# The first projections of a hybrid layer by halves of the sequence: eight plain output tiles instead of six, low parts of their weights by accumulating DMA

## The chip, the cores and the metric

One core of one Trainium2 chip runs the whole kernel. The time is device microseconds for one execution, the median of several runs. Engines are called as in the profile: PE (TensorE, matrix products), ACT (ScalarE), DVE (VectorE), POOL (GpSimd) and SP (SyncE, which here only issues loads). Each engine works through its own instructions in order and waits on semaphores. SP, ACT and POOL each issue DMAs into a queue of their own; all queues are served by the same 16 DMA engines.

## What is computed

A layer of a hybrid network on a sequence of 1024 rows of 1024 values. The change is in its beginning:

```python
c_act = jax.nn.silu(c)
mod = (c_act @ w_ada[i] + b_ada[i]).reshape(bsz, N_MOD, D_MODEL)[:, :, None, :]
shift1, scale1, gate1 = mod[:, 0], mod[:, 1], mod[:, 2]
u = rms_norm(x, ln1[i]) * (1.0 + scale1) + shift1
proj = u @ w_in
gl, cb, cc, cx, z, xbc, dt = jnp.split(proj, split_at, axis=-1)
...
g_conv, g_ssm = jnp.split(jax.nn.sigmoid(gl), 2, axis=-1)
```

`gl` are the first 2048 columns of the input projection: 16 output tiles of 128 columns, f = 0 to 15. Everything behind them (the other projections, a short convolution, a state-space scan, the output projections and an MLP) is the same in both kernels.

## The kernel before

**Data.** x comes transposed: 8 blocks k of 128 channels, each in two halves h of 512 rows of the sequence (tile `x{k}{h}`, 128x512, 256 KB). A weight tile `win[f]` is 128x1024 (512 KB), its columns k*128 to k*128+127 being the block for k. For each k, two tiles of `wada1` (512 KB each, tile `wada`) give, by a product-and-sum with the activated conditioning row on DVE (`gemv`, two records each: the custom instruction and the read of its accumulator), the scale column (q=1) and the shift column (q=0) of that k in `mcol`.

**Precision.** Each product is made of three fp32r matmuls: high weight by high u, high weight by low u, low weight by high u. `load_w` makes the high weight by a cast on ACT (`whi`) and the low one by a subtraction on DVE (`wlo`). `shift_split` does the same for u: ACT writes `uh` = x + shift, rounded; DVE writes `ul`, the rest.

**The head**, from the start to the last plain product:

- SP loads the conditioning row and the parameters, the first halves of x for all k, the first two `wada` tiles, the second halves of x, and then weights and `wada` tiles by turns. `wraw` has three buffers, `wada` eight.
- ACT squares both halves of all k, DVE adds them up, PE sums over channels (`st`), DVE takes the inverse root (the root: `rsqrt_eps` and the diagonal `sdg`), PE spreads it to all partitions, ACT copies it (`rb0`, `rb1`).
- Then for j = 0 to 7 (j is the k whose turn it is): two `gemv`, the column `s1c`, x times `s1c` times `rb` for both halves (line 46 of the kernel, `x<-x,s1c,rb`), `shift_split` for both halves, and 24 matmuls: four weight tiles f = 0 to 3, two halves, three products. Their eight sums fill the eight PSUM banks (four of pool `mm`, two each of `sx` and `st`).
- ACT writes tanh of each sum to `glt` and stores it to `gl_d`.
- Tiles f = 4 and 5 follow as plain products by `proj`, 96 matmuls.

All other tiles of the kernel that read u in pairs go by `strassen_pair`: seven half-size products of 12 matmuls each, 84 for a pair of output tiles instead of 96, with sums of weights (`s12`, `s34`) and of u (`tops_of`, made on DVE behind the head) as operands. f = 6 to 15 are five such pairs. Between f = 5 and the first pair stands the stage for dt: 32 matmuls with `wd`, 16 small ones with `sel`, an evacuation, and then the pair.

**Order.** The program is traced line by line; a list scheduler with its own estimate of durations may move instructions of an engine, also DMA issues. `tc.issue_after` holds single pieces back.

Of the kernel before, what the change touches and what calls it, by code (L numbers as in the profile page):

```python
# [37 lines left out]
def hybrid_trunk(tc, xT, par, hrows, crow, wada1, wada2, win, wdt, wco, wso, wo, wup, wdt_, wdn, out):  # L38
# [223 lines left out]
    crw = glp.tile([1, T], F32, name="crw", tag="glt")  # L262
    sp.dma_start(crw, crow)
    sp.dma_start(prm, par)
    for h in (0, 1):
# [2 lines left out]
        act.activation(ct[:, hs[h]], ps, AF.Tanh, scale=0.5)
# [31 lines left out]
    warm(4, xt[0][0])  # L300
    st = ps0.tile([P, H], F32, name="st")
    for h in (0, 1):
        acc = None
        for k in range(KT):
            sq = p0.tile([P, H], F32, name="ssq" if k else "sacc", bufs=4 if k else 2)
            act.activation(sq, xt[k][h], AF.Square)
# [4 lines left out]
        for j in range(4):
            pe.matmul(st[:, 4 * h + j:4 * h + j + 1], lhsT=acc[:, j * P:j * P + P], rhs=ones[:, 0:1],
                      start=h == j == 0, stop=True, skip_group_check=True)
    warm(2, acc)
    r = rsqrt_eps(p0, st[:, 0:8], 1.0 / T, [P, 8], "nst")
    rbs = []
    for h in (0, 1):
# [757 lines left out]
```

## Time and profile before

| | |
|---|---|
| median of 3 runs | 2132.69 us (2129.87 to 2138.76) |
| the profiled execution | 2131.68 us, span of its instructions 2129.9 us |
| PE busy | 2090.5 us, 98% of the span |
| DVE, ACT, POOL busy | 69%, 44%, 7% |
| first matmul of a plain tile starts | 32.38 us |
| first matmul of the first Strassen pair starts | 105.45 us |
| granted TensorE clock, mean of the span | 0.989 |
| accumulating DMAs in the old kernel | 36 of 256 KB, from 1818 us on |

In rows of the timeline the columns are start and busy time in us, engine, line and operation, output and inputs, shapes and count; in square brackets stands how long the engine had been idle before, and what ended it. In the table of stretches each engine has its busy time and, in brackets, its count of instructions; the last three columns are the granted clock, the share of time in which the 16 DMA engines were busy, and GB/s. Rows of DMA queues give packets, MB and the share of time of the 16 engines; q1 is SP's queue, q0 is POOL's.

### The profile page before, as it was taken

The numbers are of one execution on the slowest core, as the hardware profiler recorded it, in microseconds if no ns is written. First come the engines' busy times: TensorE is split into PE (matmuls) and PEld (weight loads), VectorE is DVE, ScalarE is ACT, GpSimd is POOL, SyncE is SP. The second block draws the span as 40 slices with busy tenths as digits, with TensorE's granted clock in tenths as the row PEclk, the third lists the DMA queues.
The fourth block names the chain that finished last, engine by engine and source line by source line (L and its number), as shares of the span: only waits on it lengthen the run. The fifth ranks groups of instructions, "written<-read, shape, count | busy, mean of one in ns | idle before, by whom it ended". The sixth has DMA issues, their size and how long they took to land.

```text
span 2129.9 us, 26252 instructions
## 1 busy us (share of the span) xinstructions
PE 2090.5 (98%) x9776; PEld 1705.4 (80%) x9776; DVE 1474.1 (69%) x2278; ACT 928.4 (44%) x1554; POOL 152.1 (7%) x242
## 2 busy tenths in 40 slices
PE   7999999999999999999999999999999999999997
PEld 4778888888888887888877788888888887888887
DVE  7866888664786757577786558746866664668774
ACT  4433333224565646364664331224544444454432
POOL 0000000000000000000000000012000001231213
PEclk8999999999999999999999999999999999999998
DMA  8126554123133223232347586453144446988922
GB/s 307 74 99 205 188 190 161 67 79 122 59 102 117 75 93 91 85 115 81 103 124 282 178 301 200 170 189 114 60 163 163 163 178 234 281 242 255 283 73 80
DMA packets 133617, 327.32 MB, mean 154 GB/s; under 512 B 12481, under 2 KB 47681, under 8 KB 131954
## 3 DMA queue, kind: packets, MB, share of 16 engines
q1 hardware_dynamic: 98978, 202.76, 29.4%
q0 software_dynamic: 22240, 87.04, 12.7%
q10 hardware_dynamic: 12272, 35.85, 4.3%
q8 instruction: 77, 1.26, 0.2%
q14 instruction: 50, 0.41, 0.1%
HBM read 253.05 MB, written 72.55 MB: 153 GB/s over the span
## 4 chain that ended last, share of the span: by engine, by line
PE 78%; issue 14%; DVE 4%; DMA 3%; ACT 1%; POOL 1%; SPq 0%; DVEq 0%; POOLq 0%; ACTq 0%
PE mm L146 20%; PE mm L112 13%; PE mm L115 13%; PE mm L113 13%; PE mm L969 11%; PE B L602 1%; PE B L607 1%; DMA wv<-in_wada 1%; PE C L624 1%; DMA y<-x_d 1%; DVE wada L293 1%; POOL wv L417 1%; PE A L579 1%; DVE ul L46 1%; DVE x L46 0%
## 5 line engine op out<-in xcount | busy, mean ns | idle before, releaser
L112 PE MATMUL mm<-uh,whi 128*128 128x512 f32 x768 | 302.9, 398 | 4.1 <-ACT uh L105 3.6
L113 PE MATMUL mm<-ul,whi 128*128 128x512 f32 x768 | 304.4, 396 | 0.0
L146 PE MATMUL mm<-t,whi 128*128 128x512 f32 x944 | 291.1, 390 | 0.6 <-DVE cq L43 0.6
L115 PE MATMUL mm<-uh,wlo 128*128 128x512 f32 x768 | 246.3, 396 | 1.9 <-DVE wlo L43 1.9
L95 ACT CAST whi<-wraw 128x1024 fp32r<-128x1024 f32 x101 | 106.0, 1050 | 261.4 <-PE mm L113 206.5
L43 DVE TENSOR_TENSOR wlo<-wraw,whi 128x1024 fp32r<-128x1024 f32 (+1 forms) x167 | 186.4, 1117 | 40.2 <-ACT whi L95 34.1
L146 PEld LDWEIGHTS mm<-t,whi 128*128 128x128 f32 x944 | 177.3, 188 | 39.2 <-DVE cq L43 2.5
L969 PE MATMUL mm<-op,whi 128*128 128x512 f32 x672 | 207.0, 389 | 0.0
L146 PE MATMUL mm<-t,wlo 128*128 128x512 f32 x472 | 183.0, 389 | 0.0
L112 PEld LDWEIGHTS mm<-uh,whi 128*128 128x128 f32 x768 | 144.4, 189 | 36.3 <-ACT uh L105 5.7
L115 PEld LDWEIGHTS mm<-uh,wlo 128*128 128x128 f32 x768 | 144.5, 189 | 32.0 <-DVE wlo L43 2.3
L113 PEld LDWEIGHTS mm<-ul,whi 128*128 128x128 f32 x768 | 145.1, 189 | 29.4 <-issue 0.9
L112 PE MATMUL mm<-ys,whi 128*128 128x512 f32 x384 | 148.7, 397 | 1.6 <-DVE gt L46 1.1
L43 DVE TENSOR_TENSOR wlo<-s,whi 128x1024 fp32r<-128x1024 f32 (+1 forms) x114 | 111.9, 994 | 54.5 <-ACT whi L151 53.6
L113 PE MATMUL mm<-ys,whi 128*128 128x512 f32 x384 | 148.5, 395 | 0.0
L969 PEld LDWEIGHTS mm<-op,whi 128*128 128x128 f32 x672 | 126.1, 188 | 26.3
L46 DVE SCALAR_TENSOR_TENSOR cacc<-raw,hw,cacc 128x1024 f32<-128x1024 f32 x96 | 122.8, 1279 | 27.6 <-ACT cacc L554 27.2
L146 PE MATMUL mm<-s,whi 128*128 128x512 f32 x448 | 138.3, 389 | 0.7 <-ACT cu L169 0.7
L969 PE MATMUL mm<-op,wlo 128*128 128x512 f32 x336 | 130.7, 389 | 0.0
L596 ACT ACTIVATE seg<-acb,acum 128x128 f32<-128x128 f32 x256 | 81.9, 392 | 99.5 <-PE B L602 91.9
L46 DVE SCALAR_TENSOR_TENSOR y<-mm,mcol,y 128x512 f32<-128x512 f32 (+1 forms) x100 | 69.6, 705 | 76.8 <-PE mm L969 41.4
L115 PE MATMUL mm<-ys,wlo 128*128 128x512 f32 x384 | 121.9, 392 | 0.0
(280 smaller groups left out, 4078.2 us busy)
## 6 DMA issues: line engine op xcount, KB each, us to landing
wraw<-in_win SPq DMA_DIRECT2D x87, 512.0 KB, 3.5
dr<-in_wdt_ SPq DMA_DIRECT2D x108, 256.0 KB, 5.1
op_d<-hp POOLq DMA_DIRECT2D x12, 1792.0 KB, 6.2
hr<-op_d POOLq DMA_DIRECT2D x42, 512.0 KB, 5.8
wv<-in_wada POOLq DMA_DIRECT2D x32, 512.0 KB, 3.7
acb<-ac_d SPq DMA_DIRECT2D x64, 256.0 KB, 4.5
wraw<-in_wup SPq DMA_DIRECT2D x32, 512.0 KB, 3.5
gt<-gl_d SPq DMA_DIRECT2D x24, 512.0 KB, 5.0
```

The lines of the kernel that those rows point to most:

```text
L43: return eng.tensor_tensor(out=o, in0=a, in1=b, op=op)
L46: return dve.scalar_tensor_tensor(out=o, in0=a, scalar=s, in1=b, op0=op0, op1=op1)
L95: act.copy(hi, raw)
L112: pe.matmul(o, lhsT=wh, rhs=h_, start=start, stop=False)
L113: pe.matmul(o, lhsT=wh, rhs=l_, start=False, stop=False)
L115: last_mm[0] = pe.matmul(o, lhsT=wl, rhs=h_, start=False, stop=stop)
L146: last_mm[0] = pe.matmul(o, lhsT=l_[:, s_], rhs=r_, start=first and k == j == 0, stop=k == 3 and j == 2, skip_group_check=True)
L293: return dve.tensor_tensor_reduce(out=w_, in0=w_, in1=cb, scale=0.5, scalar=prm[:, BADA + o:BADA + o + 1], op0=ALU.mult, op1=ALU.add, accu ...
L417: pool.dma_start(w_, wada2[i])
L579: pe.matmul(A[:, 0:P], lhsT=bf[:, cs], rhs=cf[:, cs], start=True, stop=True)
L596: act.activation(seg[:, r, :], acb[:, r, :], AF.Relu, bias=acum[:, c, hd:hd + 1], scale=-1.0)
L969: pe.matmul(o, lhsT=l_[:, c_], rhs=t[:, r_, k, :], start=first and k == j == 0, stop=k == 3 and j == 2, skip_group_check=True)
```

## The change

Eight plain tiles, f = 0 to 7, instead of six; the pairs begin at f = 8. The first halves of the sequence go first, for all eight tiles, whose eight sums fill the eight banks; the second halves of f = 4 to 7 follow k by k in the banks of f = 0 to 3 (pool `mm`), and then the second halves of f = 0 to 3. SP loads the first halves of x and leaves the second ones to step j = 1. The inverse root is taken for each half apart. The low weight is no longer a subtraction: ACT writes the rounded weight a second time, with its sign turned, and POOL adds the weight to it from HBM by an accumulating DMA. Weights of f = 4 to 7 lie in a pool of their own, `p0w`; `wada` has four buffers instead of eight. Matmuls of 128x128 on a tile of ones (`warm`) stand between PE's first steps. At the end of the head each instruction of PE, ACT, DVE and SP is tied to the one before it on its engine, so that the scheduler keeps the order of the text. `gemvs(4)` in two pairs takes the place of `gemvs(3)` in three.

```diff
+    p0w = tc.alloc_tile_pool(name="p0w", bufs=4)
...
+    def load_f(f):
+        raws.append(load_raw(win[f]))
+        pl, nh, nl, n = (wp, "whi", "wlo", None) if f < 4 else (p0w, "whx", "wlx", None)
+        whs.append(pl.tile([P, T], F32R, name=nh, bufs=n))
+        wls.append(pl.tile([P, T], F32R, name=nl, bufs=n))
+
+    def halves_of(f):
+        act.copy(whs[f], raws[f])
+        act.mul(wls[f], raws[f], -1.0)
+        pool.dma_start(wls[f], win[f], accum_op=ALU.add)
...
+    load_x(0)
+    load_ada(0)
+    for f in range(3):
+        load_f(f)
+    load_ada(1)
+    for f in range(3, 6):
+        load_f(f)
+    load_ada(2)
...
+    def part(js, fs, h, kinds=(0, 1, 2)):
...
+        for j in js:
+            for f in fs:
+                for i in kinds:
+                    w_, v_ = ((whs, uh), (whs, ul), (wls, uh))[i]
+                    pe.matmul(sps[f, h], lhsT=w_[f][:, j * P:j * P + P], rhs=v_[j][h], start=j == i == 0,
+                              stop=j == KT - 1 and i == 2, skip_group_check=True)
...
+    for j in range(1, KT):
+        scale_col(j)
+        shift_lo(j - 1, 0)
+        if j == 1:
+            for i in (0, 1):
+                part((0,), range(4), 0, (i,))
+        scaled(j, 0)
+        gemv(wa[j, 0], j)
+        shift_hi(j, 0)
+        if j == 1:
+            load_ada(3)
+            load_x(1)
+            halves_of(4)
+        if j == 2:
+            load_ada(4)
+            load_f(6)
+            load_f(7)
+            part((1,), range(4), 0, (0, 1))
+            part((0, 1), range(4), 0, (2,))
+            halves_of(5)
+        if j == 3:
+            load_ada(5)
+            part((2,), range(4), 0)
+            part((0, 1, 2), (4, 5), 0, (0, 1))
+            square(1, 0)
+            square(1, 1)
+            halves_of(6)
+        if j == 4:
+            load_ada(6)
+            part((3,), range(4), 0)
+            part((3,), (4, 5), 0, (0, 1))
+            part((0, 1, 2, 3), (4, 5), 0, (2,))
+            for k in (2, 3, 4):
+                square(1, k)
+            halves_of(7)
+            part((0, 1, 2, 3), (6,), 0, (0, 1))
+        if j == 5:
+            load_ada(7)
+            part((4,), range(6), 0)
+            part((4,), (6,), 0, (0, 1))
+            for k in (5, 6, 7):
+                square(1, k)
+            part((0, 1, 2, 3, 4), (6,), 0, (2,))
+            sums(1)
+        if j == 6:
+            part((5,), range(7), 0)
+            dg = root(1)
+        if j == 7:
+            keep_rb(spread(dg))
+            part((6,), range(7), 0)
+            part(range(7), (7,), 0)
+    shift_lo(7, 0)
+    part((7,), range(8), 0)
+    scaled(0, 1)
     for j in range(KT):
...
+        shift_hi(j, 1)
+        if j < KT - 1:
+            scaled(j + 1, 1)
+        rdy = shift_lo(j, 1)
+        if j < 4:
+            gl_half(2 * j, 0)
+        part((j,), range(4, 8), 1)
+    for f in (0, 2):
+        for f_ in (f, f + 1):
+            part(range(KT), (f_,), 1)
+    last_of = {}
+    pinned = {e_.engine for e_ in (pe, act, dve, sp)}
+    for i_ in block[head:]:
+        if i_.engine in pinned:
+            if i_.engine in last_of:
+                tc.add_manual_dep(i_, last_of[i_.engine].name, mybir.DependencyInfo(
+                    mybir.DependencyClass.NoSync, mybir.DependencyReason.DATA))
+            last_of[i_.engine] = i_
...
-    for f in range(6, 16, 2):
+    for f in range(8, 16, 2):
```

Three places show how this moves instructions. The first is SP's queue of loads. In rows before, `x_206` is the last second half of x; behind it stand weights and `wada` tiles:

```order
L281 DMA x_206<-in_xT 128x512
L88 DMA wraw<-in_win 128x1024 x2
L277 DMA wada<-in_wada 128x1024 x2
L88 DMA wraw<-in_win 128x1024
L288 DMA wx<-in_win 128x1024
L277 DMA wada<-in_wada 128x1024 x6
L88 DMA wraw<-in_win 128x1024 x3
L277 DMA wada<-in_wada 128x1024 x6
```

In the changed kernel the same queue goes on, behind the last first half of x (`x_208`), with six weights among the first three pairs of `wada`; the fourth pair follows and then the second halves (`x_195` is the first of them):

```order
L284 DMA x_208<-in_xT 128x512
L289 DMA wada<-in_wada 128x1024 x2
L88 DMA wraw<-in_win 128x1024 x3
L289 DMA wada<-in_wada 128x1024 x2
L88 DMA wraw<-in_win 128x1024 x3
L289 DMA wada<-in_wada 128x1024 x4
L284 DMA x_195<-in_xT 128x512
```

Behind the last second half (`x_209`) come `wada` of k = 4, the weights f = 6 and 7, and then `wada` of k = 5 to 7, among which the scheduler has put the weights of f = 8 to 10 of the later pairs:

```order
L284 DMA x_209<-in_xT 128x512
L289 DMA wada<-in_wada 128x1024 x2
L88 DMA wraw<-in_win 128x1024 x2
L289 DMA wada<-in_wada 128x1024
L88 DMA wraw<-in_win 128x1024
L289 DMA wada<-in_wada 128x1024 x3
L88 DMA wraw<-in_win 128x1024 x2
L289 DMA wada<-in_wada 128x1024 x2
```

All second halves of x have moved from before the weights to behind the fourth pair of `wada`. POOL's queue, which had nothing in the head, has the eight accumulating DMAs.

The second place is DVE. Before, a step of the loop over j is this (here j = 1, `x_193` and `x_194` its two halves):

```order
L293 ISA wada,mcol<-wada,cb,prm 128x1024
L293 ISA mcol 128x1
L293 ISA wada,mcol<-wada,cb,prm 128x1024
L293 ISA mcol 128x1
L46 SCALAR_TENSOR_TENSOR s1c<-mcol,prm 128x1
L46 SCALAR_TENSOR_TENSOR x_193<-x_193,s1c,rb_317 128x512
L46 SCALAR_TENSOR_TENSOR x_194<-x_194,s1c,rb_323 128x512
L46 SCALAR_TENSOR_TENSOR ul_127<-x_193,mcol,uh_111 128x512
L46 SCALAR_TENSOR_TENSOR ul_128<-x_194,mcol,uh_112 128x512
```

In the changed kernel a step has one half, `ul` of the step before it stands behind the gemv of its own, and from j = 4 on three additions of the second half's squares stand in it (here j = 4 to 5: `ul_133` is k = 4, `x_204` is k = 5):

```order
L43 TENSOR_TENSOR sacc<-sacc,ssq 128x512 x3
L305 ISA wada,mcol<-wada,cb,prm 128x1024
L305 ISA mcol 128x1
L46 SCALAR_TENSOR_TENSOR s1c<-mcol,prm 128x1
L46 SCALAR_TENSOR_TENSOR ul_133<-x_202,mcol,uh_117 128x512
L46 SCALAR_TENSOR_TENSOR x_204<-x_204,s1c,rb_338 128x512
L305 ISA wada,mcol<-wada,cb,prm 128x1024
L305 ISA mcol 128x1
L43 TENSOR_TENSOR sacc<-sacc,ssq 128x512 x3
```

So a low part of u now stands behind the load of the next k's scale tile.

The third place is ACT, from weight 1 to weight 4, two passes each (`whx` and `wlx` are those of a weight from f = 4 on; `uh_109`, `uh_111`, `uh_113` are k = 0, 1, 2):

```order
L300 CAST whi<-wraw 128x1024
L301 ACTIVATE wlo<-wraw 128x1024
L347 COPY rb_338<-st 128x512
L359 ACTIVATE uh_109<-x_194,mcol 128x512
L300 CAST whi<-wraw 128x1024
L301 ACTIVATE wlo<-wraw 128x1024
L300 CAST whi<-wraw 128x1024
L301 ACTIVATE wlo<-wraw 128x1024
L359 ACTIVATE uh_111<-x_196,mcol 128x512
L300 CAST whx<-wraw 128x1024
L301 ACTIVATE wlx<-wraw 128x1024
L359 ACTIVATE uh_113<-x_198,mcol 128x512
```

Before, the casts of the four weights stood ahead of the first `uh`, the subtractions were DVE's, and the sixteen `uh` followed one another; now the two passes for a weight stand between one `uh` and the next.

More of the change, by code (lines that the diff above doesn't have):

```diff
@@ L313, in hybrid_trunk, with root @@
                       start=h == j == 0, stop=True, skip_group_check=True)
[L314 to L317, printed above, removed]
-        dg = p0.tile([P, 4, P], F32, name="sdg", bufs=1)
-        rdy = tt(dg, ident.unsqueeze(1).broadcast_to([P, 4, P]),
-                 r[:, 4 * h:4 * h + 4].unsqueeze(2).broadcast_to([P, 4, P]), ALU.mult)
+    def root(h):
+        r = rsqrt_eps(p0, st[:, 4 * h:4 * h + 4], 1.0 / T, [P, 4], "nst")
+        dg = p0.tile([P, 4, P], F32, name="sdg", tag="ssq", bufs=2)
+        tt(dg, ident.unsqueeze(1).broadcast_to([P, 4, P]), r.unsqueeze(2).broadcast_to([P, 4, P]), ALU.mult)
+        return dg
@@ L356, in gl_evac, with scale_col, scaled @@
-    def gl_evac(f, ps):
-        t = glp.tile([P, T], F32, name="glt")
-        for h in (0, 1):
-            act.activation(t[:, hs[h]], ps[h], AF.Tanh, scale=0.5)
-        act.dma_start(gl_d[f], t)
-    for f in range(4):
-        gl_evac(f, sps[f])
+    def scale_col(j):
+        gemv(wa[j, 1], 8 + j)
+        stt(s1c[:, j:j + 1], mcol[:, 8 + j:9 + j], 1.0, prm[:, LN1 + j:LN1 + j + 1], ALU.add, ALU.mult)
+    def scaled(j, h, rb=None):
+        x_ = xt[j][h]
+        stt(x_, x_, s1c[:, j:j + 1], rbs[h] if rb is None else rb, ALU.mult, ALU.mult)
@@ new lines, in gl_half @@
+    def gl_half(f, h):
+        t = glp.tile([P, T], F32, name="glt")
+        for i in (0, 1):
+            act.activation(t[:, hs[i]], sps[f + i, h], AF.Tanh, scale=0.5)
+            act.dma_start(gl_d[f + i][:, hs[h]], t[:, hs[i]])
+    rbs = []
+    warm(9)
+    for k in range(KT):
+        square(0, k)
+    for h in (0, 1):
+        act.activation(ct[:, hs[h]], rows_c[h], AF.Tanh, scale=0.5)
+        stt(cb[:, hs[h]], ct[:, hs[h]], 1.0, rows_c[h], ALU.add, ALU.mult)
+    sums(0)
+    warm(8)
@@ new lines, in hybrid_trunk @@
+    halves_of(0)
+    dg = root(0)
+    ps = spread(dg)
+    halves_of(1)
+    warm(10)
+    scale_col(0)
+    scaled(0, 0, ps)
+    keep_rb(ps)
+    gemv(wa[0, 0], 0)
+    shift_hi(0, 0)
+    halves_of(2)
+    halves_of(3)
+    for j in range(1, KT):
+        scale_col(j)
+        shift_lo(j - 1, 0)
+        if j == 1:
+            for i in (0, 1):
+                part((0,), range(4), 0, (i,))
[44 more added lines that the diff above has]
+            part(range(7), (7,), 0)
```

108 lines of the change are left out of this document (44 added, 64 removed).

## The prediction

> **What bounds the kernel now.** I read the page's busy times first, then the table of stretches, then PE's timeline of the first 125 us, then DVE's and ACT's, and last the DMA queues.
>
> ```profile
> PE 2090.5 (98%) x9776; PEld 1705.4 (80%) x9776; DVE 1474.1 (69%) x2278; ACT 928.4 (44%) x1554; POOL 152.1 (7%) x242
> ...
> core 0: us, PE busy (x) PEld busy (x) DVE busy (x) ACT busy (x) POOL busy (x), PEclk, DMA share, GB/s
> 0.00:10.00 10.00, 7.69 (x10) 3.05 (x11) 3.69 (x9) 5.28 (x9) 1.09 (x8) 1.00 0.72 238
> 10.00:32.00 22.00, 9.49 (x27) 4.71 (x25) 16.97 (x34) 12.06 (x18) 0.00 (x0) 0.77 1.03 405
> 45.00:78.00 33.00, 33.00 (x146) 26.70 (x145) 32.08 (x55) 11.07 (x18) 0.00 (x0) 1.00 0.17 56
> 105.40:124.20 18.80, 17.85 (x74) 12.36 (x74) 5.96 (x9) 6.58 (x13) 0.00 (x0) 0.84 0.16 57
> 124.20:300.00 175.80, 175.25 (x770) 144.48 (x769) 138.34 (x212) 57.99 (x81) 13.50 (x25) 1.00 0.53 179
> 300.00:1000.00 700.00, 699.90 (x3474) 570.63 (x3473) 490.57 (x790) 330.29 (x626) 12.54 (x52) 1.00 0.32 99
> ```
>
> From 124 to 1000 us PE is never free: whatever gets PE through the head earlier ends the program earlier, one for one. In the first 32 us PE does no useful work, and DMA is the full resource there: share 1.03, 405 GB/s. PE's timeline gives the price of a matmul and the two marks that I count from:
>
> ```profile
> 32.38 0.79 PE L112 MATMUL mm<-uh,whi 128*128 128x512 f32 x2 [3.19 <-ACT uh L105]
> ...
> 44.34 0.39 PE L113 MATMUL mm<-ul,whi 128*128 128x512 f32 x1
> 44.56 0.39 PE L115 MATMUL mm<-uh,wlo 128*128 128x512 f32 x1
> ...
> 83.77 0.94 PE L115 MATMUL mm<-uh,wlo 128*128 128x512 f32 x2 [1.87 <-DVE wlo L43]
> 84.50 0.63 PE L112 MATMUL mm<-uh,whi 128*128 128x512 f32 x1
> 84.93 0.63 PE L113 MATMUL mm<-ul,whi 128*128 128x512 f32 x1
> ...
> 87.75 0.39 PE L112 MATMUL mm<-uh,whi 128*128 128x512 f32 x1
> 87.97 0.39 PE L113 MATMUL mm<-ul,whi 128*128 128x512 f32 x1
> ...
> 105.45 0.39 PE L146 MATMUL mm<-uh,whi 128*128 128x512 f32 x1
> ```
>
> A matmul follows the last by 0.227 us (146 in 33 us) at full clock, and by 0.43 us at half (84.50 to 84.93), where PE fell after a wait of 1.87 us and from which it was back at 87.75. The plain projections start at 32.38 and end at E = 105.45; from there on both kernels do the same stage for dt, then Strassen pairs.
>
> **The change: PE's count.** Before, plain tiles take 6 x 2 x 8 x 3 = 288 matmuls and the pair f=6,7 takes 84. Now eight plain tiles take 384 and that pair is gone: 12 more, 2.7 us. The pair's splits on ACT and DVE lay beside matmuls, so their loss gives nothing. At mark E the old kernel has 84 x 0.227 = 19.05 us more to do, so the new one breaks even if its plain matmuls end at 105.45 + 19.05 = **124.5 us**.
>
> **How early it could end.** PE alone: only the first halves of x (8 x 262 KB) come first. ACT's last square of them ends at 11.6; two ct and the last cb take about 2.1; the root 3.0 (23.05 to 26.02); the spread, until ACT can read it, 1.25; x, gemv and shift 2.8: first plain matmul at about 20.8, not 32.38. Plus 384 x 0.227 = 87.1, plus 2 for sums and the second spread: E = 110, a gain of 14. The durations, of ACT, DVE and PE:
>
> ```profile
> 8.18 0.58 ACT L268 ACTIVATE ct<-mm 128x512 f32<-128x512 f32 x1
> 8.65 2.94 ACT L306 ACTIVATE ssq<-x 128x512 f32<-128x512 f32 x5
> 14.96 4.66 ACT L306 ACTIVATE ssq<-x 128x512 f32<-128x512 f32 x7
> 21.50 1.04 ACT L95 CAST whi<-wraw 128x1024 fp32r<-128x1024 f32 x1 [0.23 <-DMA wraw<-in_win]
> 27.32 0.59 ACT L324 COPY rb<-st 128x512 f32<-128x512 f32 x1 [4.77 <-PE st L322]
> 50.30 1.39 ACT L105 ACTIVATE uh<-x,mcol 128x512 fp32r<-128x512 f32 x2 [4.09 <-DVE x L46]
> 8.91 0.68 DVE L46 SCALAR_TENSOR_TENSOR cb<-ct,mm 128x512 f32<-128x512 f32 x1
> 23.05 0.17 DVE L49 TENSOR_SCALAR nst<-st 128x8 f32<-128x8 f32 x1 [1.96 <-PE st L312]
> 25.33 0.69 DVE L43 TENSOR_TENSOR sdg<-ident,nst 128x512 f32<-128x512 f32 x1
> 26.26 1.02 PE L322 MATMUL st<-sdg,ones 128*128 128x512 f32 x2
> 46.91 1.28 DVE L293 CUSTOM_DVE_ANT_0 wada<-wada,cb,prm 128x1024 f32<-128x1024 f32 x1
> 48.12 1.28 DVE L293 CUSTOM_DVE_ANT_0 wada<-wada,cb,prm 128x1024 f32<-128x1024 f32 x1
> 49.52 1.41 DVE L46 SCALAR_TENSOR_TENSOR x<-x,s1c,rb 128x512 f32<-128x512 f32 x2
> 51.06 1.41 DVE L46 SCALAR_TENSOR_TENSOR ul<-x,mcol,uh 128x512 fp32r<-128x512 f32 x2
> 52.39 1.28 DVE L293 CUSTOM_DVE_ANT_0 wada<-wada,cb,prm 128x1024 f32<-128x1024 f32 x1
> ```
>
> Starts give steps: a gemv 1.21, s1c 0.2, one x half 0.77, one ul 0.66. One half step of k on DVE is 2 x 1.21 + 0.2 + 0.77 + 0.66 = 4.05 us.
>
> **Weights.** Before, the low part is a subtraction on DVE. Now ACT writes -hi with a second pass (1.05, as the cast) and an accumulating DMA from POOL adds the weight again from HBM. The 4 head subtractions (about 5 us) leave DVE; ACT gets 8 x 1.05; and the queues get 8 x 524 KB that they did not move. The only accumulating DMAs of the old kernel are the down projection's:
>
> ```profile
> wraw<-in_win SPq DMA_DIRECT2D x87, 512.0 KB, 3.5
> wlo<-in_wdt_ POOLq DMA_DIRECT2D x36, 256.0 KB, 7.2
> ...
> q0 software_dynamic: 192, 0.36, 106.2%
> ...
> q0 software_dynamic: 213, 0.41, 71.1%
> q1 hardware_dynamic: 213, 0.39, 39.4%
> ```
>
> The columns of the first two are KB and us to landing. The third is 1827 to 1829 us, where nothing but accumulation runs: 0.36 MB in 2 us, 0.18 MB/us with the engines full, against 0.405 for plain loads. So 524 KB cost 2.9 us of all DMA engines, not 1.29. The last two are 1914 to 1917, where both queues have work: 213 packets each, 0.13 MB/us each. While an accumulation is under way, SP's loads run at a third of their speed. The changed kernel's accumulations have rows of 4 KB, which no row shows. The ends are 1.29 (as a plain load) and 4.0 (the mixed 0.13 MB/us, were it all they get); I take 2.9 alone, since it is the same operation, and 0.13 when mixed, where the upper end is already in the sum.
>
> The Trainium skill, "DMA: Bandwidth & Descriptors", section "Anatomy of one DMA — SWDGE (gpsimd) path", fits a POOL DMA by 2.0 us plus its bytes at 436 GB/s, with no word on accumulation; by that, an estimate, each takes 3.2 us to land and 1.2 of the engines, and the sum would be that of the second rival below. The trace speaks against it: 256 KB took 7.2 us to land, at 0.18 MB/us.
>
> **The loads' sum.** SP's order up to the first wada tile of k=4: x 2.10, prm 0.15, four wada pairs 4.19, six weights 3.15, the other halves of x 2.10, that tile 0.52: 12.2 MB. By 10 us 2.38 MB have come (238 GB/s). The first accumulation has its data ready at 17 (weight 0 is 3.8 MB down SP's order, 13.6, and lands near 15; cast and -hi take 2.1) and starts near 18.3; SP's queue has then moved 2.38 + 8.3 x 0.405 = 5.74. Five accumulations, issued back to back, run mixed until 18.3 + 2.62/0.133 = 38.0, while SP's queue gets 2.62 more: 8.36, which is just short of wada of k=2. That pair lands at 39.7, so gemv, shift (41.6) and the halves of weight 5 (43.7) follow, and its accumulation starts at 45. SP's queue: 8.36 + 7.0 x 0.405 = 11.2 at 45, 11.7 after 3.9 us of mixing, 12.2 at 50.1; with 1.2 behind the last byte (3.5 less the data's 1.3, about half of it after the data) the tile lands at **L4 = 51.3**. As a check, without any mixing: 10 + (12.2 - 2.38)/0.405 + 6 x 2.9 + 1.2 = 52.9. DVE alone would ask for that tile at 20.0 + 3 x 4.05 = 32, so every step from k=2 on waits for its load.
>
> **From L4 to the end.** DVE's step 4 is 4.05, but ACT, in order, has copy and -hi of weight 6 (landed 2.6 after L4) until 4.7, then shift 0.7 and three squares of the second half (4.66/7 each) until 7.4, for whose adds DVE waits: step 5 starts at 8.1. Step 5: 4.05, shift 0.7, squares 2.0, add 0.7: 15.5. Step 6: 4.05 and the root (23.05 to 26.02) 3.0: 22.6. Step 7's gemv, s1c and ul of k=6: 24.7. PE then has 42 + 24 = 66 matmuls of the first halves, 15.0, and the 192 of the second halves, 43.6. E = 51.3 + 24.7 + 15.0 + 43.6 = 134.6. PE's own backlog is less: ul of k=3 at 53.4, then 144 matmuls and 1.4 for sums and spread give 87.5, and 90.7 with 3.2 us at half clock, against 91.0 by DVE. The second halves need 1.43 of DVE and at most 1.9 of ACT (a shift and two tanh of 0.6, as the rb copy) per 2.72 of PE: covered; if the evacuations (two tanh per k on ACT) were late, PE would wait for banks there. The warm-up matmuls lie in PE's waits and cost nothing unless feeds come before 20 us.
>
> So E is 134.6 against 124.5: **10 us longer.** The profiled execution took 2131.68 (span 2129.9), 1.0 below the median of 2132.69: 2141.7 by it, 2142.7 by the median, +0.5%. About 0.5% (10.7 us) is what a measurement of this kernel can tell from no change; the forecast lies on that edge.
>
> **Rivals.** *Second: accumulation costs no more than a plain load* (1.29 each): L4 = 10 + (12.2 - 2.38)/0.405 + 6 x 1.29 + 1.2 = 43.2, E = 126.5, +2 us, 2135. For: rows are longer. Against: the 0.18 MB/us with full engines. *Third, faster: plain loads go first,* accumulations fill gaps only. Then L4 = 10 + (12.2 - 2.38)/0.405 + 1.2 = 35.5, E = 118.8, a gain of 6, 2127; only with loads wholly hidden the 110 above, 2118. For: SP's queue is long before the first accumulation. Against: equal packets, 213 and 213. *Fourth, slower: PE at half clock.* If it stays there through the 57 matmuls fed by k=3 and k=4, they take 24.2 and with the sums end at 78.2; then 87 matmuls and the spread at full rate, 20.7, and 43.6: E = 142.5, +18, 2151. It decides where PE waits again in each step as long as the 1.87 us that halved it at 83.77. For: feeds come 6 to 8 us apart and 25 to 32 matmuls fill that only nearly. Against: from 84.50 it took about 3 us of work to be back.
>
> The Trainium skill, "TensorE: Matmul & The Clock Gate", section "Part 1: The HAM clock gate", puts the fall at an idle window of about 3.4 us. By that rule the 2 to 3 us waits here cost no clock, the fourth rival goes and the sum stays +10. The trace's 1.87 us disagrees, so the rival keeps its chance.
>
> **How the numbers follow.** Forecast 0.55, its own range +5 to +15 (L4 five earlier or later), so half on each side of 0.5%: same 0.28, slower 0.27. Second 0.17, same. Third 0.14: same 0.06, faster 0.08. Fourth 0.14, slower. Sum: faster 0.08, same 0.51, slower 0.41. The range is from the third's 2127, less 1, to 3 above the fourth's 2151.
>
> **What will show it.** First plain matmul near 21; casts and -hi of eight weights on ACT; wlo landing over 6 us after its issue; q0 and q1 even in 18 to 38 us; wada of k=4 near 51 with DVE waiting for DMA before its gemv; PE idle and at half clock for most of 21 to 50; the last plain matmul near 135, and everything behind it as before. It is wrong if wada of k=4 lands before 40 (accumulations cheaper or behind), if PE is full from 30 us, or if second halves wait for banks.

## The result, and the profile after

The changed kernel takes 2143.35 us (median of 7 runs, 2140.78 to 2145.73) against 2132.65 us before (7 runs, 2129.87 to 2138.76): a ratio of 1.005, 95% interval 1.004 to 1.0061. That is 10.7 us slower; the forecast was 10, and 2142.7. The profiled execution has a span of 2143.0 us against 2129.9. The page's busy times first:

```profile
PE 2095.8 (98%) x9836; PEld 1714.6 (80%) x9836; DVE 1460.0 (68%) x2270; ACT 933.5 (44%) x1559; POOL 159.4 (7%) x250
```

PE's share is the same 98%; the share says nothing of where the time went. The table of stretches, with the columns as before, does:

```profile
20.00:30.00 10.00, 6.33 (x30) 4.11 (x28) 5.84 (x10) 7.71 (x9) 2.25 (x4) 0.83 1.05 272
30.00:40.00 10.00, 1.76 (x4) 1.48 (x5) 2.94 (x6) 0.00 (x0) 0.84 (x1) 0.50 1.06 272
40.00:50.00 10.00, 10.00 (x37) 7.76 (x36) 5.80 (x10) 4.38 (x6) 0.86 (x1) 0.82 1.05 353
50.00:60.00 10.00, 5.08 (x13) 3.93 (x13) 5.33 (x9) 4.39 (x7) 0.86 (x1) 0.69 1.02 388
```

From 20 to 60 us PE is busy for 23 of 40 us, the clock is down to 0.50 in one stretch, and the DMA engines are full (1.02 to 1.06) while they move only 272 GB/s in the first two stretches, not 405. PE's timeline shows the waits:

```profile
23.17 0.73 PE L375 MATMUL mm<-uh,whi 128*128 128x512 f32 x2 [0.57 <-ACT uh L359]
...
38.24 0.79 PE L375 MATMUL mm<-ul,whi 128*128 128x512 f32 x1 [9.75 <-DVE ul L46]
...
49.70 0.39 PE L375 MATMUL mm<-uh,whi 128*128 128x512 f32 x1
55.01 0.80 PE L375 MATMUL mm<-ul,whi 128*128 128x512 f32 x1 [4.92 <-DVE ul L46]
...
60.71 0.39 PE L375 MATMUL sx<-uh,whx 128*128 128x512 f32 x1
```

And DVE's timeline shows what they hang on:

```profile
36.03 1.28 DVE L305 CUSTOM_DVE_ANT_0 wada<-wada,cb,prm 128x1024 f32<-128x1024 f32 x1 [9.75 <-DMA wada<-in_wada]
52.81 1.28 DVE L305 CUSTOM_DVE_ANT_0 wada<-wada,cb,prm 128x1024 f32<-128x1024 f32 x1 [4.52 <-DMA wada<-in_wada]
...
76.38 0.75 DVE L46 SCALAR_TENSOR_TENSOR ul<-x,mcol,uh 128x512 fp32r<-128x512 f32 x1
```

The two waits of PE, 9.75 and 4.92 us, are DVE's two waits for `wada` of k = 2 (36.03) and of k = 4 (52.81): the low part of u of the step before stands behind that gemv. After each, PE runs at half clock for some 6 us (38.24 to about 44.3, 55.01 to 60.71). Behind 55.01 it is not idle until the plain matmuls are done. The mark I use for that end, E, is the first matmul of the stage for dt, in the rows of tile `wd`:

```profile
L509 PE MATMUL st<-uh,wd x16: 387/397/398, 135.6 to 143.9; 128*64 128x512 f32 x16
```

A later mark is the first transpose of `acum`, behind all pairs that read u, in the rows of that tile:

```profile
L643 PEld LDWEIGHTS st<-ident,acum x8: 94/97/97, 503.8 to 509.2; 128*32 128x32 f32 x8
```

So E is 135.6, and `acum` is at 503.8. In the changed kernel dt follows right behind the last plain matmul. In the kernel before, four matmuls of the first pair stand between the two, so its mark is the first of these, 105.45, and break-even is 105.45 + 19.05 = 124.5. Its `acum` is at 490.9:

```profile
L530 PEld LDWEIGHTS st<-ident,acum x8: 94/97/97, 490.9 to 496.3; 128*32 128x32 f32 x8
```

So the head is 11.1 us longer, the pairs behind it 1.8, the rest of the program 0.2: 13.1 between the two profiled spans. The medians differ by 10.7 only, since the profiled execution of the changed kernel is 1.5 us above its median and that of the kernel before 1.0 below. The 2.0 us behind the head are no more than two executions of one kernel differ by.

### The profile page after: what moved, and what is told of

Its sections match the earlier page's. It is cut to its first block, busy times and chain, and to the rows that moved or that the text cites. A ratio compares the mean times of both kernels' runs of the same rounds, so it can differ in the third digit from the quotient of the medians.

```text
span 2143.0 us, 26399 instructions
## 1 busy us (share of the span) xinstructions
PE 2095.8 (98%) x9836; PEld 1714.6 (80%) x9836; DVE 1460.0 (68%) x2270; ACT 933.5 (44%) x1559; POOL 159.4 (7%) x250
## 4 chain that ended last, share of the span: by engine, by line
PE 85%; issue 8%; DMA 3%; DVE 2%; POOL 1%; ACT 0%; SPq 0%; DVEq 0%; POOLq 0%; ACTq 0%
PE mm L146 20%; PE mm L113 15%; PE mm L115 15%; PE mm L112 15%; PE mm L1082 9%; PE mm L375 2%; PE B L715 2%; PE B L720 2%; PE C L737 1%; DMA wada<-in_wada 1%; DMA hr<-op_d 1%; PE st L375 1%; PE sx L375 1%; PE A L692 1%; POOL wv L530 1%
## 5 line engine op out<-in xcount | busy, mean ns | idle before, releaser
L146 PE MATMUL mm<-t,whi 128*128 128x512 f32 x912 | 280.7, 390 | 3.7 <-DVE cq L43 3.7
L113 PE MATMUL mm<-ul,whi 128*128 128x512 f32 x704 | 278.7, 396 | 0.0
L112 PE MATMUL mm<-uh,whi 128*128 128x512 f32 x704 | 278.7, 396 | 0.0
L115 PE MATMUL mm<-uh,wlo 128*128 128x512 f32 x704 | 223.2, 395 | 0.0
L43 DVE TENSOR_TENSOR wlo<-wraw,whi 128x1024 fp32r<-128x1024 f32 (+1 forms) x160 | 178.6, 1116 | 40.1 <-ACT whi L95 34.0
L146 PEld LDWEIGHTS mm<-t,whi 128*128 128x128 f32 x912 | 170.7, 188 | 41.1 <-DVE cq L43 5.7
L146 PE MATMUL mm<-t,wlo 128*128 128x512 f32 x456 | 176.8, 389 | 0.0
L115 PEld LDWEIGHTS mm<-uh,wlo 128*128 128x128 f32 x704 | 132.2, 188 | 27.2 <-issue 0.2
L113 PEld LDWEIGHTS mm<-ul,whi 128*128 128x128 f32 x704 | 132.4, 188 | 26.7 <-issue 0.9
L112 PEld LDWEIGHTS mm<-uh,whi 128*128 128x128 f32 x704 | 132.3, 188 | 26.5 <-issue 0.2
```

Source lines behind the costliest of these rows:

```text
L43: return eng.tensor_tensor(out=o, in0=a, in1=b, op=op)
L112: pe.matmul(o, lhsT=wh, rhs=h_, start=start, stop=False)
L113: pe.matmul(o, lhsT=wh, rhs=l_, start=False, stop=False)
L115: last_mm[0] = pe.matmul(o, lhsT=wl, rhs=h_, start=False, stop=stop)
L146: last_mm[0] = pe.matmul(o, lhsT=l_[:, s_], rhs=r_, start=first and k == j == 0, stop=k == 3 and j == 2, skip_group_check=True)
```

## The experiments

The theory at the start: accumulating DMAs run at less than half of a load's rate and share the engines evenly with SP's queue; `wada` tiles come late, and DVE, ACT and PE behind them set the end. Rivals: only the bytes of the second read count; loads are hidden, the chain of DVE and ACT sets the end. Each run was timed beside the kernel before on the same chip. All marks in one table: E in us (for the kernel before, its break-even of 124.5), then the time from E to the `acum` mark, then from there to the end of the span, and the ratio with its 95% interval. The marks are those of one profiled execution each. The expectations of runs 6, 8 and 10 compare with 365 to 365.5 us to `acum` for the kernel before; that count goes from the start of dt there, 106.4, and is 0.9 us too short.

| kernel | E | to `acum` | rest | ratio to before |
|---|---|---|---|---|
| before | 124.5 | 366.4 | 1639.0 | |
| changed | 135.6 | 368.2 | 1639.2 | 1.005 (1.004 to 1.0061) |
| 1 plain writes | 129.9 | 371.5 | 1637.2 | 1.0024 (1.0011 to 1.0037) |
| 2 no second read | 124.6 | 373.7 | 1640.7 | 1.0033 (1.0022 to 1.0045) |
| 3 subtraction on POOL | 137.1 | 373.0 | 1642.9 | 1.0101 (1.0073 to 1.0128) |
| 4 second halves last | 133.1 | 372.0 | 1637.1 | 1.0049 (1.0034 to 1.0064) |
| 5 low part of u first | 135.3 | 367.2 | 1644.3 | 1.0093 (1.0076 to 1.011) |
| 6 two `wv` | 134.8 | 370.2 | 1639.2 | 1.0055 (1.004 to 1.007) |
| 7 subtraction on DVE | 133.9 | 374.1 | 1640.9 | 1.0067 (1.0052 to 1.0082) |
| 8 four edits | 135.2 | 368.9 | 1637.4 | 1.0054 (1.0039 to 1.0069) |
| 9 not tied | 134.8 | 374.7 | 1645.7 | 1.0074 (1.005 to 1.0098) |
| 10 no second read, two `wv` | 124.7 | 368.3 | 1643.1 | 1.0001 (0.9987 to 1.0014) |
| 11 early feed | 129.6 | 367.7 | 1640.6 | 1.003 (1.0017 to 1.0043) |
| 12 root hidden | 120.2 | 370.6 | 1644.6 | 1.0011 (1.0 to 1.0023) |

**1. Plain writes.**

```diff
-        pool.dma_start(wls[f], win[f], accum_op=ALU.add)
+        pool.dma_start(wls[f], win[f])
```

> The eight DMAs of POOL's queue are issued at the same places and move the same 524 KB each, but write instead of adding; the low part of the weight is then the whole weight (the subtraction is left out). Theory (an accumulation costs 2.9 us of the DMA engines, a plain load 1.29, and that makes wada of k=4 late): that tile lands near 43 to 45 instead of 52.8, the plain matmuls end at 126.5 to 128 instead of 135.6, time 2134 to 2136, 8 us less than the changed kernel. Rival 1 (the second read of the weights costs its bytes, adding costs nothing more): tile at 52.8, no change, 2143. Rival 2 (the chain of DVE and ACT and PE's half clock set the end, loads are hidden): POOL's DMAs land earlier, but the end stays within 2 us of 135.6, 2141 to 2143.

`wada` of k = 4 is there at 47.2 instead of 52.8, and E is 129.9:

```profile
47.21 1.28 DVE L305 CUSTOM_DVE_ANT_0 wada<-wada,cb,prm 128x1024 f32<-128x1024 f32 x1 [4.37 <-DMA wada<-in_wada]
```

The queues (packets, MB, share of time) from 32 to 34 us in the changed kernel:

```profile
q0 software_dynamic: 79, 0.26, 66.0%
q1 hardware_dynamic: 81, 0.29, 38.9%
```

and in the same two microseconds of this one:

```profile
q1 hardware_dynamic: 113, 0.40, 54.5%
q0 software_dynamic: 112, 0.40, 53.8%
```

In both, the two queues get about the same number of packets; with accumulation each gets 0.26 to 0.29 MB in 2 us, without it 0.40, the engines being full both times. So adding, as against writing, costs 5.6 us at the tile and 5.7 at E: rival 1 falls, and so does rival 2. The gain is smaller than the 8 expected.

**2. No second read at all.**

```diff
-        pool.dma_start(wls[f], win[f], accum_op=ALU.add)
```

> The eight accumulating DMAs are left out, and nothing takes their place: the low part of a weight stays the rounded weight with its sign turned. Theory: wada of k=4 lands at 35.5 to 37 (10 + 9.82 MB / 0.405 + 1.2, and up to 1.5 more as measured in the changed kernel), the plain matmuls end at 119 to 121, time 2126 to 2129, 15 us less than the changed kernel and 5 less than the one before. Rival 1 (bytes alone): the eight reads are worth 8 x 1.29, of them 6 ahead of that tile: 7.7 us less, end at 128, 2135. Rival 2 (chain of DVE and ACT): end within 2 us of 135.6, 2141 to 2143.

The tile is there at 41.8, not at 35.5 to 37, and E is 124.6, not 119 to 121:

```profile
41.81 1.28 DVE L304 CUSTOM_DVE_ANT_0 wada<-wada,cb,prm 128x1024 f32<-128x1024 f32 x1 [1.82 <-DMA wada<-in_wada]
```

Reading the weights a second time costs 5.4 us more at the tile and 5.3 at E. Together the accumulating DMAs cost 11.0 us of E, nearly all of the 11.1 that the head lost: without them it would be level with the head before (124.6 against 124.5), and no faster. What ACT's second passes cost, which this run keeps, was not tried apart. The theory's 15 left something out. It is in the list of SP's waits of this run (us in total, times, longest):

```profile
SPq L88 <- ACT wlo L301: 8.2, 3, 4.8
SPq L289 <- DVE mcol L304: 5.2, 4, 2.3
```

and in its table of stretches:

```profile
20.00:25.00 5.00, 2.83 (x18) 1.89 (x16) 4.97 (x9) 4.30 (x6) 0.00 (x0) 1.00 0.37 116
25.00:30.00 5.00, 2.51 (x6) 1.46 (x6) 0.66 (x3) 3.30 (x4) 0.00 (x0) 0.53 0.95 322
```

SP's queue stands still for buffers: the fourth weight waits until ACT is through with the first (three `wraw` buffers), `wada` until DVE has used the earlier ones (four). With nothing else to move, the engines are busy for 0.37 of 20 to 25 us. In the changed kernel SP's queue waits for the first weights as long (8.7 us), but the engines are full all the same with accumulations (1.06 in 20 to 25 us). And the run shows a second thing: E fell by 11.0 us, the span by 4.0. Behind the head 5.5 of them were lost again by the `acum` mark, and 1.5 behind it.

**3. Subtraction on POOL.**

```diff
-        act.mul(wls[f], raws[f], -1.0)
-        pool.dma_start(wls[f], win[f], accum_op=ALU.add)
+        tt(wls[f], raws[f], whs[f].bitcast(F32), ALU.subtract, eng=pool)
```

> The low part is a subtraction again, on POOL (about 3 us each by its 1.5 us for half the width), from the loaded weight; ACT's second pass and the accumulating DMAs are gone. Theory: loads run alone, but a weight buffer (three) comes free only behind POOL's subtraction, so the fourth to sixth weight are asked for at about 19, 22 and 25 and wada of k=2 behind them lands near 30, wada of k=4 near 39; the plain matmuls end near 122 and the time is near 2130, 13 less than the changed kernel and within 0.3% of the one before. Rival 2 (chain of DVE and ACT): ACT loses 8.4 us of passes, of which about 3 stood in the chain behind k=4: end near 132, 2140. A third theory (POOL's subtraction slows DVE down beside it): gemv and x take longer than 1.28 and 0.77 each, and the end comes later than 126.

E is 137.1: the third theory holds. POOL's timeline:

```profile
16.16 4.65 POOL L43 TENSOR_TENSOR wlo<-wraw,whi 128x1024 fp32r<-128x1024 f32 x2 [14.50 <-ACT whi L300]
28.30 2.53 POOL L43 TENSOR_TENSOR wlo<-wraw,whi 128x1024 fp32r<-128x1024 f32 x1 [7.49 <-ACT whi L300]
```

and DVE's beside it:

```profile
15.59 0.16 DVE L43 TENSOR_TENSOR nst<-nst 128x4 f32<-128x4 f32 x1
...
16.18 2.36 DVE L43 TENSOR_TENSOR nst<-nst 128x4 f32<-128x4 f32 x1
...
27.85 0.75 DVE L46 SCALAR_TENSOR_TENSOR ul<-x,mcol,uh 128x512 fp32r<-128x512 f32 x1
28.51 2.87 DVE L46 SCALAR_TENSOR_TENSOR x<-x,s1c,rb 128x512 f32<-128x512 f32 x1
```

The same addition of 4 columns takes 0.16 us alone and 2.36 when POOL's subtraction starts beside it; an x of 0.75 takes 2.87. Each of the seven subtractions that start before 55 us stops DVE for 2.0 to 2.2 us. This standstill is not alone in setting E: SP's queue also waits 14.9 us for weight buffers that POOL's subtractions hold, and what each of the two costs was not tried apart. POOL is no free place for this work beside a DVE that is in the chain.

**4. Second halves of x last.**

```diff
         if j == 1:
-            load_x(1)
...
         if j == 5:
             load_ada(7)
+            load_x(1)
...
+    for k in range(KT):
+        square(1, k)
+    sums(1)
+    dg = root(1)
+    keep_rb(spread(dg))
+    part(range(KT), (7,), 0)
```

> The second halves of x are loaded behind the last wada tile instead of ahead of wada of k=4; their squares, sums, root and spread come in one piece behind the first halves' last step, and the eighth tile's first half behind them. The accumulating DMAs stay. Theory: wada of k=4 comes 2.1 MB / 0.405 = 5.2 us earlier, near 47.6, the steps of DVE lose three additions each, wada of k=7 lands near 68, the second halves near 72, root and spread are done near 79, the eighth tile's 24 matmuls and the second halves' 192 follow: end at 127 to 129, time 2135 to 2137. Rival 2 (chain of DVE and ACT by itself): the additions and the root stand in one piece that PE has to wait for: end later than 135.6, over 2143.

E is 133.1: 2.5 us earlier, not 7 to 9. PE waits 10.6 us for the low part of k = 1 (until 36.8), which stands on DVE behind the gemv of k = 2; from there on PE is never idle until the second root. From the list of its waits, and DVE's wait for that tile:

```profile
PE mm L375 <- DVE ul L46: 10.6, 1, 10.6
PE st L342 <- DVE sdg L43: 3.0, 1, 3.0
34.57 1.29 DVE L305 CUSTOM_DVE_ANT_0 wada<-wada,cb,prm 128x1024 f32<-128x1024 f32 x1 [10.64 <-DMA wada<-in_wada]
```

So it is no longer the landing of k = 4 that counts but that of k = 2, and PE's own backlog behind it: between 21 and 37 us PE got 9 matmuls (eight of k = 0, one of k = 1), and what it is not fed there it cannot make up. (In the changed kernel it is 9 as well between 23 and 38 us, not the 16 that the expectation of run 5 counts.) The loads of k = 4 and later came earlier to no use.

**5. Low part of u ahead of the next gemv.**

```diff
-        scale_col(j)
         shift_lo(j - 1, 0)
+        scale_col(j)
```

> The low part of u of k-1 is issued ahead of the gemv of k on DVE instead of behind it; nothing else changes. Theory (PE's backlog counts: from 23 to 38 us it runs 16 matmuls and then waits 9.75 us for the low part of k=1, which stands behind the load of wada of k=2; the low part of k=3 stands behind wada of k=4): the 9.75 us wait ends near 28, PE has the matmuls of k=1 and k=3 done by the time the late tiles land, and the end of the plain matmuls is set by the low part of k=6 near 74 on DVE: end at 132 to 133.5 instead of 135.6, time 2141 to 2142. Rival (only the landing of wada of k=4 and what follows it on DVE and ACT count): end at 135 or later, no change, 2143.

The 9.75 us wait is gone, and E is 135.3: the rival's number, though not for its reason. PE now runs into the next thing that is late, the accumulated low weights, as the list of its waits shows:

```profile
PE mm L375 <- DMA wlo<-in_win: 6.7, 2, 3.6
PE mm L375 <- DVE ul L46: 2.7, 1, 2.7
```

In the order of the text, the low products of k = 0 and 1 stand ahead of k = 2, and PE waits for two of the accumulations until 34.5 and 38.2. The run is slower than the changed kernel by more than its profile accounts for (the profiled execution was its shortest): left open.

**6. Two `wv` buffers.** In the pairs behind the head POOL loads a weight of the later gemvs into one tile; DVE uses it, and only then the next load starts.

```diff
-            w_ = pe1.tile([P, T + 32], F32, name="wv", bufs=1)[:, 0:T]
+            w_ = pe1.tile([P, T + 32], F32, name="wv", bufs=2)[:, 0:T]
...
-        cy = tp_.tile([P, H], F32, name="cy") if keep else cq
+        cy = tp_.tile([P, H], F32, name="cy", bufs=1) if keep else cq
```

> The tile wv, into which POOL loads the 32 conditioning weights of the later gemvs, has two buffers instead of one (cy has one instead of two, to make room). The head is unchanged: end of the plain matmuls at 135.6. Theory of the second loss (in the pairs behind the head DVE waits for the one wv buffer to be loaded, 30 us in 16 waits, and what stands behind it on DVE, the sum cq, makes PE wait): from the end of the plain matmuls to the first transposes of acum 368.2 us fall to 365 or less, as in the kernel before (365.5 on the same count), time near 2140. Rival (the few us behind the head are scatter, or come from DVE's load as such): stays at 368, 2143.

From E to `acum` it takes 370.2 us, not 365: no gain in the changed kernel. The 1.8 us that its pairs lose against before are not shown to come from this buffer.

**7. Subtraction on DVE,** as in the kernel before.

```diff
-        act.mul(wls[f], raws[f], -1.0)
-        pool.dma_start(wls[f], win[f], accum_op=ALU.add)
+        tt(wls[f], raws[f], whs[f].bitcast(F32), ALU.subtract)
```

> The low part is a subtraction on DVE as in the kernel before; ACT's second pass and the accumulating DMAs are gone. Theory: loads are as in the run without accumulation (wada of k=4 near 42, a little earlier for weight buffers that come free sooner), DVE is then the bound with 4 more subtractions of 1.2 us behind that tile: end of the plain matmuls at 126 to 130 (124.6 without any subtraction), and of the 6 to 9 us gained two thirds are lost again in the pairs behind, by the single wv buffer: time 2138 to 2141. Rival (nothing is lost behind the head): 2134 to 2137.

E is 133.9: 9.3 later than without any subtraction, where four of 1.2 were expected. In the tied order DVE also waits ahead of four of the eight 1.6 to 1.7 us for ACT's cast, so the subtractions ahead of the tile of k = 4 may not be hidden either; how the 9.3 divide was not worked out. So the accumulating DMA and DVE's subtraction cost this head about the same: 11.0 and 9.3 us (run 7 also does without ACT's second pass, which run 2 keeps).

**8. Edits 4, 5, 6 and 7 together.**

> Four edits together: subtraction on DVE, second halves of x loaded last with their squares and root in one piece, low part of u ahead of the next gemv, two wv buffers. Theory: DVE's eight steps of 4.05 and eight subtractions of 1.2 from 18 on end near 62, squares, root and spread near 72, end of the plain matmuls at 118 to 124; with two wv buffers nothing is given back: 365 us to the transposes of acum, 1639 behind them: span 2122 to 2128, time 2124 to 2130, 3 to 9 us less than the kernel before. Rival (the loss behind the head is not the wv buffer): the end of the plain matmuls as said, time 2132 to 2137.

E is 135.2. Up to k = 5 the steps on DVE take about 7 us, with those waits for casts, where 5.25 were expected, and PE is not filled before 50 us. The pairs behind take 368.9 us, against 374.1 in run 7.

**9. Not tied.**

```diff
-    for i_ in block[head:]:
-        if i_.engine in pinned:
...
```

> The tie between instructions of one engine is left out, so the scheduler orders the head by its own estimates: the second halves of x are loaded ahead of weights 3 to 5 and of wada of k=2, their squares and sums stand between the first steps, everything else is as in the changed kernel. Theory (what lands late sets the end): wada of k=2 comes up to 5.2 us later, weight 3 too, no load ahead of wada of k=4 is saved: end of the plain matmuls at 136 to 141, time 2144 to 2149. Rival (the tied order itself costs, since instructions that are ready stand behind ones that wait): end before 134, time below 2142.

E is 134.8, below what was expected: weight 3 is late (PE waits 10.3 us for a cast, until 37.3), but `wada` of k = 2, which the scheduler set ahead of weights 3 to 5, is there at 32.3, not later than 36.0, and from 37 to 65 us PE is fed (then it waits 5.1 us for a shift). The tie moves the end of the head by less than 1 us; the whole program is not faster without it.

**10. No second read and two `wv` buffers.** Runs 2 and 6 joined.

> The accumulating DMAs are left out (low parts of the weights stay the rounded weights with their sign turned) and wv has two buffers. Alone, the first gave an end of the plain matmuls of 124.6 but lost 8 us of the 11 behind it (373.7 us to the transposes of acum instead of 365.5). Theory (the loss is DVE's wait for the one wv buffer ahead of the sum cq): 367 to 370 us, time 2134 to 2137. Rival (whatever PE gains in the head it waits for again, since DVE as such is the bound in these pairs): 372 or more, time 2139 to 2142.

The head is that of run 2 (124.7), and the pairs now take 368.3 us instead of 373.7; the ratio falls from 1.0033 to 1.0001. PE's waits from 130 to 520 us in run 2:

```profile
PE mm L146 <- DVE cq L43: 8.0, 5, 2.6
```

and in this one:

```profile
PE mm L146 <- DVE glt L46: 2.0, 1, 2.0
PE mm L146 <- DVE cq L43: 0.8, 2, 0.7
```

And DVE's wait for the buffer in the 150 us from the first z pair on, in the kernel before:

```profile
DVE wv L293 <- DMA wv<-in_wada: 14.4, 9, 2.2
```

in the changed kernel:

```profile
DVE wv L305 <- DMA wv<-in_wada: 18.7, 9, 2.6
```

in run 2:

```profile
DVE wv L304 <- DMA wv<-in_wada: 23.4, 10, 3.8
```

and in run 10:

```profile
DVE wv L304 <- DMA wv<-in_wada: 7.7, 6, 2.4
```

So the rival falls: with two buffers DVE's wait for `wv` and PE's wait for `cq` shrink together, and 5.4 of the 7.3 us by which run 2's pairs were longer than before are back. (With two buffers the scheduler also orders DVE otherwise in these pairs; the two were not tried apart.) With one pair fewer between head and z pairs, 22 of the 32 gemvs are left for them in the changed kernel and in run 2, 19 before, 14 in run 10.

The loss is not tied to a faster head, though. PE's wait for `cq` from 130 to 520 us is this in the kernel before:

```profile
PE mm L146 <- DVE cq L43: 0.6, 1, 0.6
```

and this in the changed kernel:

```profile
PE mm L146 <- DVE cq L43: 3.7, 4, 1.7
```

In runs 3, 4, 7 and 9, whose E is within 2.5 us of the changed kernel's, it is 6.5 to 8.0 us, and the pairs take 372.0 to 374.7. In the five runs with two buffers (6, 8, 10, 11, 12) it is 0.8 to 2.7 us, and the pairs take 367.7 to 370.6. Why the same instructions in the same order wait longer in run 2 than in the changed kernel is not settled; the landing of `wv` has a longest of 6.9 us there, 5.6 in the changed kernel.

**11. Early feed.** The low part is made by what the runs so far suggest: subtraction on DVE for weights 0 to 3, where it can stand in gaps; accumulation for 4 to 7, but late; no weight waits for a buffer, since 0 to 3 are loaded into the tiles of x's second halves, which are still empty.

```diff
+        if f < 4:
+            raws.append([xt[2 * f + i][1] for i in (0, 1)])
+            for i in (0, 1):
+                sp.dma_start(raws[f][i], win[f][:, hs[i]])
...
+    def lo_of(f):
+        if f < 4:
+            for i in (0, 1):
+                tt(wls[f][:, hs[i]], raws[f][i], whs[f].bitcast(F32)[:, hs[i]], ALU.subtract)
+        else:
+            act.mul(wls[f], whs[f].bitcast(F32), -1.0)
+            pool.dma_start(wls[f], win[f], accum_op=ALU.add)
```

> A head with the same matmuls and another order of loads: weights 0 to 3 are loaded into the tiles of the second halves of x and subtracted on DVE; weights 4 to 7 keep the accumulating DMA, but it is issued after step 5, when SP's queue is nearly done, from the rounded weight; no load waits for a weight buffer; the second halves of x come last; high products of tiles 4 to 7 fill PE's waits, their low products come last; wv has two buffers. Theory (late loads, then DVE's steps): wada of k=2 near 27 instead of 36, of k=4 near 34 instead of 52.8, DVE is the bound with eight steps of about 5, four subtractions of 1.2, the additions 5.5 and the root 3: second halves start near 73 to 76, end of the plain matmuls at 117 to 122; 366 to 370 us to the transposes of acum: span 2122 to 2131, time 2124 to 2133, 3 to 10 less than the kernel before. Rival (DVE's hand-over to ACT and back in each step is the bound whatever the loads do): steps of 7 us as with subtractions on DVE alone, end at 128 or later, time over 2137.

E is 129.6, 6 us earlier than in the changed kernel, and above the expected 117 to 122. DVE is through with the last low part at 57; but PE, full from 31 us, reaches the second half's sums only at 76, and then waits for the root (3.0) and for copy and shift (2.2) with nothing left to do.

**12. Root hidden.**

```diff
+    sums(1)
+    part(r8, (4, 5), 0, (2,))
+    dg = root(1)
+    ps = spread(dg)
+    part(r8, (6, 7), 0, (2,))
+    keep_rb(ps)
```

> The head of the run before it with four moves: the second halves of x are loaded ahead of the last two pairs of wada instead of behind them, the accumulating DMAs are issued one step later, casts of weights 2 to 5 stand earlier on ACT, and the sums and the spread of the second root stand on PE between the low products of tiles 4 to 7 instead of behind them. In that run PE was never idle from 31 to 79.6 us and then waited 5.3 us for root and copy at half clock. Theory (PE's own work is the bound there): the waits at 79 to 84 go, and 1 to 3 us of those before 31: end of the plain matmuls at 119 to 124 instead of 129.6, 368 us to the transposes of acum: span 2127 to 2133, time 2129 to 2135, level with the kernel before or up to 5 us less. Rival (the accumulations, all issued behind 50 us, land too late for the low products): PE waits for them, end at 126 or later, time over 2135.

E is 120.2, 15.4 us earlier than in the changed kernel. The list of PE's waits from 20 us to E:

```profile
PE mm L392 <- ACT uh L376: 2.7, 2, 1.9
PE sx L392 <- ACT whx L309: 1.3, 2, 0.8
PE mm L392 <- DVE ul L46: 0.7, 2, 0.3
```

It takes 2135.70 us (12 runs) against 2132.67 (17): 1.0011, 1.0 to 1.0023. That is better than the changed kernel, and it does not beat the one before: of 4.3 us gained in the head against before, 4.2 are lost by the `acum` mark, and the part behind it is 5.6 longer. That part, identical work, lies between 1637.1 and 1645.7 us over these kernels. PE's waits in it add up to 13.1 us in the kernel before and to 19.7 in this one, enough for the 5.6; what makes them longer was not looked for.

## Why the prediction was right, step by step

- **First plain matmul:** 20.8 forecast, 23.2 measured. ACT's squares end at 12.6, not 11.6, since two buffers `ssq` make three of them wait for DVE's additions; the wait from there to the root is 0.9 longer, root and spread 0.4. It cost nothing: PE waited for loads afterwards in any case.
- **Rates:** mixed, 0.133 MB/us per queue forecast, 0.13 to 0.145 measured (32 to 34 us), with rows of 4 KB too. The Trainium skill, "DMA: Bandwidth & Descriptors", section "Anatomy of one DMA — SWDGE (gpsimd) path", gave an estimate of 3.2 us to landing; the trace disagrees: 7.0 to 12.7 us in the changed kernel, and 5.3 to 8.0 without accumulation (run 1), in both cases beside SP's loads.
- **L4:** 51.3 forecast, 52.8 measured. From there, step 5 at +8.1 (measured +7.9), step 6 at +15.5 (+15.5), step 7 at +22.6 (+22.2), end of the low part of k = 6 at +24.7 (+24.3).
- **The end:** 134.6 forecast, 135.6 measured. The sum went by DVE's chain (91.0) and had PE's backlog just below it (87.5, or 90.7 with half clock). It was the backlog: behind 55.01 PE never waits. Run 4 bears that out: loads of k = 4 and later that come earlier move E by 2.5 us only. Run 5 does not test it, since PE waits there for the accumulations instead. That the two sums were 0.3 us apart is why the forecast of E holds with the wrong one of them.
- **The queues** were to be even from 18 to 38 us. They were from 30 to 38; in 28 to 30 POOL's queue moved 19 packets and SP's 157. The first five accumulations were not issued back to back but at 17.8, 19.7, 25.3, 27.2 and 30.0, since ACT had the copy of `rb` and the first shift, until 23.0, ahead of the third weight's cast, and SP's queue stopped for weight buffers meanwhile. That the second tile of k = 2 was used at 39.8, as forecast (39.7), looks like luck in part: SP's queue stopped, which the forecast left out, and the accumulations came later than it had them.
- **Second rival** (E = 126.5): in run 1, where the writes are plain, 129.9. **Third:** with no accumulations beside the loads at all, 124.6 (run 2), where it had 118.8. The step that failed in both is the loads' sum, "10 + bytes / 0.405": it lets SP's queue run without a stop, and the queue stops for buffers. In the forecast the fault did not show, because the engines had accumulations to move in these stops; that was luck.
- **Fourth:** half clock came twice, for about 6 us each, not through both steps; the first was followed by another wait and cost nothing.
- **"Whatever gets PE through the head earlier ends the program earlier, one for one"** was wrong. It held for the change: 11.1 us at E, 10.7 in the medians. Of the 11.0 us that run 2 gained, 4.0 reached the end of the profiled span; of the 15.4 of run 12, 7.6. In the row quoted for 124 to 300 us DVE was busy for 138 of 176 us, and its waits for `wv` were in the trace of before: 14.4 us that PE did not yet feel.
- **Second halves** never wait for banks, as forecast. Everything behind the head "as before" was off by 2.0 us.

## What to carry to other kernels

A transfer that takes work off an engine is paid where the queues are full: here eight accumulations of 512 KB took 11 us from a head whose loads were already the full resource, half of it for the second read, half for adding. Before pricing a load by bytes and rate, look in the list of the queue's waits for buffers: a stop there can hide behind the very thing that you want to remove. And when the time gained at the first bound does not reach the end, look for the next wait that had been just short of showing: here two buffers in place of one, with the order that the scheduler made of them, took 5.4 us off a later stage (run 10 against run 2). They gave nothing in the changed kernel (run 6), so one trial of such a buffer settles little.
